# First modulations from whole fp32 weights as the stationary operand, with the conditioning rows prepared at the beginning

## Chip, cores and metric

One core of a Trainium2 chip. The metric is the device time of one execution in microseconds; the kernel before takes 1435.6 us, the median of 3 runs (1433.16 to 1436.79). Engines are named as in the profile: PE (matrix engine; PEld are its weight loads), DVE, ACT, POOL, and SP, which here only issues transfers.

## The reference, cut to what matters

Two layers over 256 latent tokens and 256 context tokens of width 1024. Each layer begins with a norm modulated by six vectors that come from the conditioning:

```python
def adaln(cond, w_ada, b_ada):
    return jnp.split(jax.nn.silu(cond) @ w_ada + b_ada, 6, axis=-1)

def modulate(x, shift, scale):
    return rms_norm(x) * (1.0 + scale) + shift

# per layer l
sh1, sc1, g1, sh2, sc2, g2 = adaln(c, w_ada[l], b_ada[l])
csh1, csc1, cg1, csh2, csc2, cg2 = adaln(c_ctx, w_ada[l], b_ada[l])
... = project(modulate(ctx, csh1, csc1), w_in[l])
... = project(modulate(x, sh1, sc1), w_in[l])
# three mixers (gating MLP, windowed attention, gated linear attention), merged, then
x_new = x + g1 * merge_branches(a_out, b_out, c_out, gates, w_br[l], w_o[l])
x_new = x_new + g2 * sq_relu_ffn(modulate(x_new, sh2, sc2), w_ff1[l], w_ff2[l])
```

`w_ada[l]` is 1024 x 6144. The change concerns the first 2048 of these columns in layer 0 (shift `sh1` and scale `sc1`), for both conditioning vectors.

## The kernel before

**Weights.** All weights stream from one packed tensor `wpk` in chunks of at most 128 x 1024 fp32 (512 KB), in the order of `layer_chunks`; `START_ORDER` is its beginning. A "B" chunk holds two 128-row blocks of 512 columns, an "A" chunk eight 128-row blocks of one column tile of 128. `emit_chunk` issues the transfer on SP's queue into a raw tile (two rings of four, the second used by the chunks of `START_RAW`), casts it to fp32r on ACT (`whi`, L296) and takes the rest on DVE or POOL (`wlo`, L298). `chunk` hands a split chunk to the matmuls and emits `SPLIT_AHEAD` = 2 further ones. Activations are split in the same way, and a product is three matmuls (hi x hi, hi x lo, lo x hi). Every matmul has the one line 316, every transpose line 320.

**Order.** The orders of PE and SP are those in which the program is written. A small planner writes them: `run` advances the main generator, which adds each matmul's estimated time to `clk`, and interleaves spawned generators when `clk` has reached their due time (the `LAT` table). ACT, DVE and POOL are ordered by Tile's scheduler.

**The start of layer 0** (`start`). SP issues the two x transfers, then raw chunks. `norm_start0` squares x on ACT, adds on DVE, sums over partitions on PE with `ones`, takes the power on POOL, spreads it by PE, and multiplies x by it in place (L1304, half on DVE, half on POOL). Meanwhile `ada_group` computes 512 columns of the modulation at a time from four "B" chunks: the stationary operand is `csil` (128 x 4: the two silu vectors, each split), the moving one the split weights with 512 columns, 16 matmuls a group, 64 in all. The result has four rows; `ada_rows` combines and transposes it with the small matrix `comb` (four fp32 matmuls, eight instructions a group) and adds the bias. Groups 0 and 1 give the first half of shift and scale, 2 and 3 the second. `half(i)` waits for them and for both norms, then modulates and splits four of the eight blocks of h (`nt`, L1361 and L1363; `h`, L367 and L368). Then the first projections (`kvp`, `qp`) run: kv and the two context query tiles with the first half of h, the same with the second, then the two latent query tiles. After that stand `load_constants2`, `layer_params` (masks, norms' gains, rope tables) and, last, `cond_rows`: it loads both conditioning vectors to all partitions (`sil`, 1 MB) and takes their silu (tanh on ACT, L467, two DVE steps, L468 and L469) through two tiles of the raw ring.

**Later modulations.** All other columns of both layers come from `ada_task`, background work on DVE: a row-wise product of `w_adaT` with `sil`, summed (L490).

**The query chain** (`q_chain`) takes a projected query tile through a square (ACT), a sum (DVE L665), a power (POOL L375), two products, a split (L676, L677), and PE's transposes, which stand in PE's order between the projections.

Of the kernel before, what the change touches and what calls it, by code (L numbers as in the profile page):

```python
# [16 lines left out]
P = 128  # L17
# [20 lines left out]
def layer_chunks(l):  # L38
# [38 lines left out]
    for kind, g, js in FFN_ORDER:  # L77
# [4 lines left out]
        else:  # L82
            for _ in range(2 if g == 3 and not last else 1):
# [8 lines left out]
             (1, 3, range(4)), (2, 2, None), (1, 3, range(4, 8)), (2, 3, None)]  # L92
LAT_FIRST = 4
# [50 lines left out]
def shape_constants():  # L144
    t = np.arange(SEQ)
    nf = HD // 4
    freqs = (10000.0 ** (-np.arange(nf, dtype=np.float32) / nf)).astype(np.float32)
    cos = np.zeros((SEQ, HD), np.float32)
    sin = np.zeros((SEQ, HD), np.float32)
    for half, pos in ((0, t // GRID_W), (1, t % GRID_W)):  # L150
        ang = pos.astype(np.float32)[:, None] * freqs[None, :]
        c, s = np.cos(ang), np.sin(ang)
        o = half * 32
        cos[:, o:o + nf] = c
        cos[:, o + nf:o + 2 * nf] = c
# [27 lines left out]
    comb = np.array([[1, 0], [0, 1], [1, 0], [0, 1]], np.float32)  # L183
    return {"rope": np.ascontiguousarray(rope.astype(np.float32)),
            "consts": np.ascontiguousarray(big), "comb": comb,
            "tri": np.ascontiguousarray(tri.transpose(1, 0, 2).reshape(P, -1))}
# [4 lines left out]
       "ada": 1.51, "x": 0.54, "half": 1.35, "kv_lat": 6.0, "kv_ctx": 4.5, "kv_out": 0.7, "q_lat": 7.5,  # L191
# [3 lines left out]
       "c_out": 1.5, "acc": 3.5, "rstd": 2.5, "rstd0": 0.77, "mod": 2.0,  # L195
# [11 lines left out]
class Builder:  # L207
# [76 lines left out]
    def emit_chunk(self):  # L284
# [8 lines left out]
        nc.sync.dma_start(raw[:, :n], src)  # L293
        hi = self.wp.tile([P, 1024], F32R, tag="whi", name="whi")
# [96 lines left out]
    def load_constants(self):  # L391
# [9 lines left out]
        self.comb = cp.tile([4, 2], F32, name="comb")  # L401
        nc.scalar.dma_start(self.comb, a["comb"])
# [44 lines left out]
    def cond_setup(self):  # L447
        nc, cp, a = self.nc, self.cp, self.a

        cT = self.tr(name="cT")[:, :16].rearrange("p (k c) -> p k c", c=2)  # L450
        nc.sync.dma_start(cT, a["condT"])
        th = self.tr(name="cth")[:, :16]
# [31 lines left out]
    def ada_task(self, l, n, conds):  # L484
# [3 lines left out]
        for c in conds:  # L488
            junk = self.bp.tile([P, D], BF16, tag="b2k", name="junk")
            nc.vector.scalar_tensor_tensor(junk, raw, 1.0, self.sil[:, c], op0=ALU.mult, op1=ALU.mult,  # L490
# [793 lines left out]
    def norm_start0(self, s, x, R):  # L1284
# [11 lines left out]
        yield self.lat("x")  # L1296
# [5 lines left out]
        for i in range(2):  # L1302
            xh = x[:, i * 4:i * 4 + 4, :]
            (nc.vector if i == 0 else nc.gpsimd).tensor_tensor(  # L1304
                xh, xh, R.unsqueeze(1).to_broadcast([P, 4, SEQ]), op=ALU.mult)
        self.flags.add(f"R{s}")

    def ada_group(self, g):
        c0 = ADA_START[g]
        ps = self.sc_bank()  # L1310
        for kc in range(4):
            if kc > 0:
                yield
            w = self.chunk(("B", "w_ada", c0, 512, 2 * kc))
            for kk in range(2):
                k = 2 * kc + kk
                for q in range(2):
                    self.mm(ps[:4, :], self.csil[:, k, :], w[q][:, kk * 512:(kk + 1) * 512],
                            start=(k == 0 and q == 0), stop=(k == KT - 1 and q == 1))
        rows = self.tp.tile([4, 512], F32, tag="t2k", name="adarow")  # L1320
        self.nc.scalar.copy(rows, ps[:4, :])
        self.spawn(self.ada_rows(g, rows), self.lat("ada"))

    def ada_rows(self, g, rows):

        nc = self.nc
        out = self.sc_bank()
        ov = out[:, :8].rearrange("p (n c) -> p n c", c=2)
        for j in range(4):
            self.mm(ov[:, j, :], rows[:, j * P:(j + 1) * P], self.comb, True, True)  # L1330
        n0 = ADA_START[g] // P
        o = self.ada[0][:, :, n0:n0 + 4]
        b = self.bada[:, 0, n0:n0 + 4].unsqueeze(1).to_broadcast([P, 2, 4])
        nc.vector.tensor_tensor(o, ov.rearrange("p n c -> p c n"), b, op=ALU.add)
        if n0 >= 8:
            nc.vector.tensor_scalar(o, o, 1.0, None, op0=ALU.add)
        self.flags.add(f"ada{g}")
        yield 0.0

    def start(self, h, kv_ready, q_ready):  # L1340
# [5 lines left out]
        ada = [self.ada_group(g) for g in range(4)]  # L1346
        for s in range(2):
            nc.sync.dma_start(x[s], self.a["xT"][s])
# [3 lines left out]
        yield from ada[0]  # L1352
        yield from ada[1]
        def half(i):
            yield from self.until(f"ada{2 * i}", f"ada{2 * i + 1}", "R0", "R1")
# [12 lines left out]
        self.spawn(half(0), 0.0)  # L1368
        yield from ada[2]
        yield from ada[3]  # L1370
# [20 lines left out]
        self.spawn(half(1), 0.0)  # L1391
# [5 lines left out]
        self.load_constants2()  # L1397
        self.layer_params(0)
# [5 lines left out]
        self.cond_rows()  # L1404
# [63 lines left out]
```

## Time and profile before

| | |
|---|---|
| median of 3 runs | 1435.6 us (1433.16 to 1436.79) |
| profiled execution | 1438.17 us, its span 1436.4 us |
| mean granted clock of PE | 0.979 |
| PE / PEld busy | 1366.7 (95%) / 1192.3 us |
| DVE / ACT / POOL busy | 991.7 (69%) / 661.6 (46%) / 451.7 us (31%) |
| moved by DMA | 214.08 MB, mean 149 GB/s |

The span runs from the first to the last instruction; what lies around it is 1.8 us here. Busy time of an engine is the union of its instructions. A granted clock of 1.00 is 2.4 GHz and 0.50 is 1.2 GHz. In a row of the timeline the first number is the start, the second the length of a merged run of equal instructions, and brackets tell the idle time before it and who ended it. In a table of stretches each engine's busy time is followed by its count of instructions.

### The profile page before, as it was taken

The numbers are of one execution on the slowest core, as the hardware profiler recorded it, in microseconds if no ns is written. First come the engines' busy times: TensorE is split into PE (matmuls) and PEld (weight loads), VectorE is DVE, ScalarE is ACT, GpSimd is POOL, SyncE is SP. The second block draws the span as 40 slices with busy tenths as digits, with TensorE's granted clock in tenths as the row PEclk, the third lists the DMA queues.
The fourth block names the chain that finished last, engine by engine and source line by source line (L and its number), as shares of the span: only waits on it lengthen the run. The fifth ranks groups of instructions, "written<-read, shape, count | busy, mean of one in ns | idle before, by whom it ended". The sixth has DMA issues, their size and how long they took to land.

```text
span 1436.4 us, 21724 instructions
## 1 busy us (share of the span) xinstructions
PE 1366.7 (95%) x8272; PEld 1192.3 (83%) x8272; DVE 991.7 (69%) x1669; ACT 661.6 (46%) x1095; POOL 451.7 (31%) x288
## 2 busy tenths in 40 slices
PE   4968998998999999999999999999999999999999
PEld 2757787877788889888887888987799999999999
DVE  7776678876576768768885566886875665864453
ACT  5755455643223335442332323555556635565443
POOL 2030002213112334553342424431110245465554
PEclk8989999998999999999999999999999999999999
DMA  7621112321354455444556656442144335556554
GB/s 301 230 73 45 59 64 68 118 103 45 118 175 162 150 196 182 158 140 172 205 207 213 216 193 215 165 149 89 48 138 149 104 118 161 180 162 202 181 178 131
DMA packets 60391, 214.08 MB, mean 149 GB/s; under 512 B 7230, under 2 KB 8510, under 8 KB 59648
## 3 DMA queue, kind: packets, MB, share of 16 engines
q1 hardware_dynamic: 58696, 209.51, 43.5%
q10 hardware_dynamic: 1592, 3.20, 0.7%
q8 instruction: 65, 1.06, 0.3%
q14 instruction: 38, 0.31, 0.1%
HBM read 211.63 MB, written 1.05 MB: 148 GB/s over the span
## 4 chain that ended last, share of the span: by engine, by line
PE 41%; DVE 10%; issue 3%; DMA 3%; ACT 1%; POOL 0%; SPq 0%; DVEq 0%; ACTq 0%; POOLq 0%
PE mm L316 37%; DVE junk L490 4%; DMA adaw<-w_adaT 3%; PE sm L316 2%; DVE wlo L298 1%; PE sc L316 1%; PE sm L320 1%; DVE acc L507 1%; ACT whi L296 0%; DVE h L546 0%; DVE x L1259 0%; DVE f L1215 0%; DVE mx L717 0%; DVE nt L541 0%; ACT gab L820 0%
## 5 line engine op out<-in xcount | busy, mean ns | idle before, releaser
L296 ACT CAST whi<-raw 128x1024 fp32r<-128x1024 f32 (+1 forms) x312 | 322.9, 1039 | 524.1 <-PE mm L316 419.0
L316 PE MATMUL mm<-h,whi 128*128 128x512 f32 (+2 forms) x2112 | 515.1, 336 | 1.7 <-ACT h L1177 0.8
L316 PEld LDWEIGHTS mm<-h,whi 128*128 128x128 f32 x2112 | 361.7, 192 | 40.8 <-DVE h L1178 1.1
L298 DVE TENSOR_TENSOR wlo<-raw,whi 128x1024 fp32r<-128x1024 f32 (+1 forms) x215 | 286.7, 1336 | 107.9 <-ACT whi L296 106.7
L316 PE MATMUL mm<-h,wlo 128*128 128x512 f32 (+2 forms) x1056 | 352.4, 334 | 0.0
L298 POOL TENSOR_TENSOR wlo<-raw,whi 128x1024 fp32r<-128x1024 f32 x97 | 240.1, 2475 | 346.7 <-ACT whi L296 340.9
L316 PE MATMUL mm<-f,whi 128*128 128x256 f32 (+1 forms) x1152 | 257.2, 319 | 0.0
L490 DVE SCALAR_TENSOR_TENSOR junk<-adaw,sil 128x1024 bf16<-128x1024 f32 x128 | 184.9, 1472 | 57.0 <-DMA adaw<-w_adaT 56.8
L316 PEld LDWEIGHTS mm<-h,wlo 128*128 128x128 f32 x1056 | 202.2, 192 | 19.2
L316 PEld LDWEIGHTS mm<-f,whi 128*128 128x128 f32 x1152 | 192.0, 191 | 15.2
L316 PE MATMUL mm<-f,wlo 128*128 128x256 f32 (+1 forms) x576 | 183.8, 319 | 2.9 <-DVE wlo L298 2.4
L316 PE MATMUL mm<-whi,h 128*128 128x512 f32 (+2 forms) x544 | 172.0, 386 | 0.0
L316 PEld LDWEIGHTS mm<-f,wlo 128*128 128x128 f32 x576 | 109.7, 190 | 11.7 <-DVE wlo L298 3.7
L316 PEld LDWEIGHTS mm<-whi,h 128*128 128x128 f32 x544 | 103.7, 199 | 16.3
L316 PE MATMUL mm<-wlo,h 128*128 128x512 f32 (+2 forms) x272 | 102.9, 378 | 0.4 <-DVE wlo L298 0.4
L1214 POOL TENSOR_TENSOR ffr<-ffr 128x512 f32<-128x512 f32 (+1 forms) x64 | 71.5, 1118 | 46.1 <-ACT f L1213 37.5
L1215 DVE TENSOR_TENSOR f<-ffr,f 128x512 fp32r<-128x512 f32 (+1 forms) x64 | 56.2, 886 | 29.7 <-POOL ffr L1214 29.5
L1259 DVE SCALAR_TENSOR_TENSOR x<-mm,ada,x 128x256 f32<-128x256 f32 x96 | 43.6, 478 | 42.5 <-PE mm L316 42.3
L383 POOL TENSOR_SCALAR gx<-gx 128x512 f32<-128x512 f32 (+1 forms) x14 | 14.0, 1000 | 183.2 <-ACT gx L382 183.1
L316 PE MATMUL mm<-m,whi 128*128 128x256 f32 x384 | 69.5, 283 | 0.0
L316 PEld LDWEIGHTS mm<-wlo,h 128*128 128x128 f32 x272 | 54.2, 199 | 8.1 <-DVE wlo L298 1.1
L1061 POOL TENSOR_TENSOR mg<-mg,gth 128x512 f32<-128x512 f32 (+1 forms) x28 | 34.4, 1230 | 84.1 <-DVE gth L1060 84.1
(291 smaller groups left out, 1828.5 us busy)
## 6 DMA issues: line engine op xcount, KB each, us to landing
raw<-wpk SPq DMA_DIRECT2D x304, 512.0 KB, 3.8
adaw<-w_adaT SPq DMA_DIRECT2D x80, 512.0 KB, 3.8
raw<-wpk SPq DMA_DIRECT2D x8, 288.0 KB, 2.9
x<-xT SPq DMA_DIRECT2D x2, 1024.0 KB, 6.9
x<-xT ACTq DMA_DIRECT2D x2, 1024.0 KB, 6.9
sil<-cond SPq DMA_DIRECT2D x1, 1024.0 KB
out<-x ACTq DMA_DIRECT2D x8, 128.0 KB, 1.7
trif<-tri SPq DMA_DIRECT2D x2, 384.0 KB, 2.9
```

The costliest lines, as they stand in the source:

```text
L296: nc.scalar.copy(hi[:, :n], raw[:, :n])
L298: eng.tensor_tensor(lo[:, :n], raw[:, :n], hi[:, :n].bitcast(F32), op=ALU.subtract)
L316: self.nc.tensor.matmul(out, lhsT, rhs, start=start, stop=stop)
L320: self.nc.tensor.transpose(out, src, self.ident)
L383: nc.gpsimd.tensor_scalar(x2[:, :n], x2[:, :n], 0.044715, 1.0, op0=ALU.mult, op1=ALU.add)
L490: nc.vector.scalar_tensor_tensor(junk, raw, 1.0, self.sil[:, c], op0=ALU.mult, op1=ALU.mult, accum_out=self.ada[l][:, c, n:n + 1])
L507: nc.vector.tensor_tensor(acc, acc, sq, op=ALU.add)
L1061: (nc.vector if m is not None and n >= KT - 2 else nc.gpsimd).tensor_tensor(mg, mg, th[:, :nt], op=ALU.add)
L1214: nc.gpsimd.tensor_tensor(r[:, :nt], r[:, :nt], r[:, :nt], op=ALU.mult)
L1215: nc.vector.tensor_tensor(lo, r[:, :nt], hi.bitcast(F32), op=ALU.subtract)
L1259: nc.vector.scalar_tensor_tensor(x[s][:, n], ps[:, s * SEQ:(s + 1) * SEQ], self.ada[l][:, s, 40 + n:41 + n], x[s][:, n], op0=ALU.mult, op1 ...
```

## The change

1. The first 2048 columns of the modulation arrive as sixteen "A" chunks, one column tile each. They are not split: `emit_chunk` keeps the raw tile. The raw weights become the stationary operand (128 x 128 fp32), `csil` in fp32 (two columns) the moving one: eight matmuls a tile, and the result stands already with columns on partitions. `ada_rows` and `comb` go.
2. `ada_half` takes eight tiles for the first half of shift and scale and eight for the second; each adds its bias in two DVE steps.
3. SP issues two raw chunks ahead of each x transfer.
4. x is scaled by its norm in `half(i)`, four blocks at a time and on DVE alone.
5. `cond_rows`, `load_constants2` and `layer_params` are called after the first eight tiles; `cond_rows` works in four pieces of 512 through other tiles, and its factor 0.5 moves into `ada_task`.
6. The planner's due times for these steps are new.

```diff
-ADA_START = (0, 1024, 512, 1536)
+ADA_START = ((0, 1, 2, 3, 8, 9, 10, 11), (4, 5, 6, 7, 12, 13, 14, 15))
-START_ORDER = [("B", "w_ada", c0, 512, kk) for c0 in ADA_START[:2] for kk in range(0, KT, 2)]
-START_ORDER += [("B", "w_ada", c0, 512, kk) for c0 in ADA_START[2:] for kk in range(0, KT, 2)]
+START_ORDER = [("A", "w_ada", 0, n * P) for ns in ADA_START for n in ns]
...
         nc.sync.dma_start(raw[:, :n], src)
+        if self.specs[i][1] == "w_ada":
+            self.split[i] = raw
+            return
...
     def cond_setup(self):
-        self.csil = self.big([P, KT, 4], F32R, name="csil")
-        self.split_hl(self.csil[:, :, 0:2], self.csil[:, :, 2:4], thv)
+        self.csil = thv
...
     def cond_rows(self):
         for c in range(2):
-            th = self.wp.tile([P, D], F32, tag="raw", bufs=4, name="silt")
-            nc.scalar.activation(th, self.sil[:, c], AF.Tanh, scale=0.5)
-            nc.vector.scalar_tensor_tensor(th, th, 1.0, self.sil[:, c], op0=ALU.add, op1=ALU.mult)
-            nc.vector.tensor_scalar(self.sil[:, c], th, 0.5, None, op0=ALU.mult)
+            for i in range(2):
+                v = self.sil[:, c, i * 512:(i + 1) * 512]
+                th = self.trb(name="silt")
+                nc.scalar.activation(th, v, AF.Tanh, scale=0.5)
+                nc.vector.scalar_tensor_tensor(v, th, 1.0, v, op0=ALU.add, op1=ALU.mult)
...
     def norm_start0(self, s, x, R):
         nc.scalar.copy(R, R0[:, :SEQ])
-        for i in range(2):
-            xh = x[:, i * 4:i * 4 + 4, :]
-            (nc.vector if i == 0 else nc.gpsimd).tensor_tensor(
-                xh, xh, R.unsqueeze(1).to_broadcast([P, 4, SEQ]), op=ALU.mult)
...
-    def ada_group(self, g):
-    def ada_rows(self, g, rows):
+    def ada_half(self, i):
+        nc = self.nc
+        ps = self.sc_bank()
+        ov = ps[:, :16].rearrange("p (n c) -> p n c", c=2)
+        for j, n in enumerate(ADA_START[i]):
+            w = self.chunk(("A", "w_ada", 0, n * P))
+            for k in range(KT):
+                self.mm(ov[:, j], w[:, k * P:(k + 1) * P], self.csil[:, k], k == 0, k == KT - 1)
+            self.clk += ADA_TILE
+            yield
+        for j in (0, 4):
+            n0 = ADA_START[i][j]
+            o = self.ada[0][:, :, n0:n0 + 4]
+            b = self.bada[:, 0, n0:n0 + 4].unsqueeze(1).to_broadcast([P, 2, 4])
+            r = ov[:, j:j + 4].rearrange("p n c -> p c n")
+            if j == 0:
+                nc.vector.tensor_tensor(o, r, b, op=ALU.add)
+            else:
+                nc.vector.scalar_tensor_tensor(o, r, 1.0, b, op0=ALU.add, op1=ALU.add)
+        self.flags.add(f"ada{i}")
...
     def start(self, h, kv_ready, q_ready):
         for s in range(2):
+            for _ in range(2):
+                self.emit_chunk()
             nc.sync.dma_start(x[s], self.a["xT"][s])
...
         def half(i):
-            yield from self.until(f"ada{2 * i}", f"ada{2 * i + 1}", "R0", "R1")
+            yield from self.until(f"ada{i}", "R0", "R1")
+            for s in range(2):
+                xh = x[s][:, i * 4:i * 4 + 4, :]
+                nc.vector.tensor_tensor(xh, xh, Rs[s].unsqueeze(1).to_broadcast([P, 4, SEQ]), op=ALU.mult)
...
+        for i in range(2):
+            yield from self.ada_half(i)
+            self.spawn(half(i), self.lat("ada"))
+            if i == 0:
+                self.cond_rows()
+                self.load_constants2()
+                self.layer_params(0)
         yield from self.need("half0")
```

The calls of `ada[0]` to `ada[3]`, and the later calls of `load_constants2`, `layer_params` and `cond_rows`, go from their old places.

## Rows read from the trace of the kernel before

**Rows 1.** The page: busy time of each engine, share of the span, instructions

```profile
PE 1366.7 (95%) x8272; PEld 1192.3 (83%) x8272; DVE 991.7 (69%) x1669; ACT 661.6 (46%) x1095; POOL 451.7 (31%) x288
```

**Rows 2.** Busy time by stretch: us, each engine (instructions), granted clock, DMA share, GB/s

```profile
2.00:47.66 45.66, 27.72 (x105) 12.80 (x105) 34.26 (x45) 28.01 (x40) 8.03 (x4) 0.89 0.79 291
47.66:79.30 31.64, 31.21 (x177) 27.01 (x175) 24.65 (x52) 21.88 (x41) 1.39 (x2) 1.00 0.53 191
79.30:92.30 13.00, 6.01 (x19) 5.07 (x19) 8.43 (x17) 4.58 (x10) 5.85 (x2) 0.61 0.29 98
```

**Rows 3.** Groups by line, 0 to 47.4 us: count, busy us, mean ns, idle before

```profile
L298 DVE TENSOR_TENSOR wlo<-raw,whi 128x1024 fp32r<-128x1024 f32 x16 | 19.3, 1220 | 3.2 <-ACT whi L296 3.2
L296 ACT CAST whi<-raw 128x1024 fp32r<-128x1024 f32 x16 | 16.3, 1043 | 12.7 <-PE sc L316 12.7
L1304 DVE TENSOR_TENSOR x<-x,Rb 128x1024 f32<-128x1024 f32 x2 | 6.7, 3402 | 0.0
```

**Rows 4.** Timeline of the first 40 us: start, length, engine, line, operation, count

```profile
1.18 0.90 SPq L1348 DMA_DIRECT2D x<-xT  x2
7.04 2.19 ACT L1290 ACTIVATE sq<-x 128x512 f32<-128x512 f32 x4 [3.14 <-DMA x<-xT]
11.73 2.93 ACT L296 CAST whi<-raw 128x1024 fp32r<-128x1024 f32 x3
```

**Rows 5.** Timeline, weight loads of 128x128 fp32 (PEld), then matmuls with two moving columns

```profile
15.80 0.76 PEld L316 LDWEIGHTS sm<-ones,sq 128*128 128x128 f32 x3
...
16.66 0.55 PEld L316 LDWEIGHTS sm<-ones,sq 128*128 128x128 f32 x2
...
30.20 1.86 PE L316 MATMUL sc<-comb,adarow 4*128 4x2 f32 x8
32.00 0.59 PE L316 MATMUL sc<-whi,csil 128*4 128x512 f32 x1
```

**Rows 6.** Timeline of PE, loads of 128x128 with two moving columns, in dense work

```profile
340.33 0.25 PE L316 MATMUL sm<-ind,gh 128*128 128x2 f32 x1
...
340.89 0.25 PE L316 MATMUL sm<-ind,gl__2775 128*128 128x2 f32 x1
```

**Rows 7.** Busy time by stretch, two stretches around rises of the clock

```profile
30.70:34.12 3.42, 3.42 (x13) 1.89 (x13) 1.65 (x3) 0.87 (x2) 0.00 (x0) 0.50 0.92 274
354.84:358.40 3.56, 3.56 (x9) 2.81 (x9) 3.53 (x15) 0.76 (x2) 0.00 (x0) 0.50 0.00 0
```

**Rows 8.** Timeline of PE, small matmuls and then dense ones, 351 to 359 us

```profile
351.82 3.09 PE L316 MATMUL sm<-v,glaw 64*128 64x128 f32 x16
354.84 1.22 PE L316 MATMUL mm<-h,whi 128*128 128x512 f32 x2
...
358.42 0.44 PE L316 MATMUL mm<-h,wlo 128*128 128x512 f32 x1
```

**Rows 9.** Timeline around the first kv matmul and of the second half of h

```profile
47.66 0.30 PE L316 MATMUL mm<-whi,h 128*128 128x288 f32 x1
...
50.75 1.05 PE L316 MATMUL sc<-comb,adarow 4*128 4x2 f32 x8
53.52 0.17 DVE L1336 TENSOR_SCALAR ada<-ada 128x8 f32<-128x8 f32 x1
...
58.66 2.50 DVE L368 TENSOR_TENSOR h<-nt,h 128x512 fp32r<-128x512 f32 x4
```

**Rows 10.** Timeline, the first context q chain and PE's wait for it

```profile
77.12 0.68 DVE L665 TENSOR_REDUCE qss<-qt 128x8 f32<-128x512 f32 x1
...
79.56 4.21 POOL L375 TENSOR_TENSOR rq<-rq,mhalf 128x8 f32<-128x8 f32 x1 [6.77 <-DVE rq L374]
...
86.32 1.94 PE L320 MATMUL sm<-ident,qt 128*128 128x128 f32 x8 [6.99 <-DVE qt L677]
```

**Rows 11.** Groups by line of DVE, 73.4 to 82.5 us

```profile
L468 DVE SCALAR_TENSOR_TENSOR silt<-silt,sil 128x1024 f32<-128x1024 f32 x2 | 2.4, 1220 | 0.0
L469 DVE TENSOR_SCALAR sil<-silt 128x1024 f32<-128x1024 f32 x2 | 1.4, 686 | 0.0
```

More of the change, by code (lines that the diff above doesn't have):

```diff
@@ L182, in shape_constants @@
     ], 1).astype(np.float32)
-    comb = np.array([[1, 0], [0, 1], [1, 0], [0, 1]], np.float32)
     return {"rope": np.ascontiguousarray(rope.astype(np.float32)),
-            "consts": np.ascontiguousarray(big), "comb": comb,
+            "consts": np.ascontiguousarray(big),
             "tri": np.ascontiguousarray(tri.transpose(1, 0, 2).reshape(P, -1))}
 LAT = {
-       "ada": 1.51, "x": 0.54, "half": 1.35, "kv_lat": 6.0, "kv_ctx": 4.5, "kv_out": 0.7, "q_lat": 7.5,
+       "ada": 0.5, "x0": 6.5, "x1": 11.0, "half": 3.0, "kv_lat": 6.0, "kv_ctx": 4.5, "kv_out": 0.7, "q_lat": 7.5,
        "q_ctx": 5.0, "q_out": 1.0, "s_lat": 4.2, "s_ctx": 3.4, "p_lat": 2.6, "p_ctx": 2.0, "po": 1.0,
@@ L194 @@
        "g2": 1.5, "g3": 1.0, "g1s": 3.0, "g4": 1.8, "1g4": 7.0, "states": 8.0, "on": 4.0, "c": 1.2,
-       "c_out": 1.5, "acc": 3.5, "rstd": 2.5, "rstd0": 0.77, "mod": 2.0,
+       "c_out": 1.5, "acc": 3.5, "rstd": 2.5, "rstd0": 3.0, "mod": 2.0,
        "0states": 15.2, "0s_lat": 2.83, "0mix": 1.68, "1acc": 4.66, "1s_lat": 3.91, "0g2": 1.26, "0va0": 5.01,
@@ L400, in load_constants @@
         nc.vector.memset(self.mhalf, -0.5)
-        self.comb = cp.tile([4, 2], F32, name="comb")
-        nc.scalar.dma_start(self.comb, a["comb"])
         self.ada = [cp.tile([P, 2, 48], F32, name=f"ada{l}") for l in range(DEPTH)]
@@ L448, in cond_setup @@
         nc, cp, a = self.nc, self.cp, self.a
-        cT = self.tr(name="cT")[:, :16].rearrange("p (k c) -> p k c", c=2)
+        cT = cp.tile([P, 16], F32, name="cT").rearrange("p (k c) -> p k c", c=2)
         nc.sync.dma_start(cT, a["condT"])
-        th = self.tr(name="cth")[:, :16]
+        th = cp.tile([P, 16], F32, name="cth")
         thv = th.rearrange("p (k c) -> p k c", c=2)
@@ L489, in ada_task @@
             junk = self.bp.tile([P, D], BF16, tag="b2k", name="junk")
-            nc.vector.scalar_tensor_tensor(junk, raw, 1.0, self.sil[:, c], op0=ALU.mult, op1=ALU.mult,
+            nc.vector.scalar_tensor_tensor(junk, raw, 0.5, self.sil[:, c], op0=ALU.mult, op1=ALU.mult,
                                            accum_out=self.ada[l][:, c, n:n + 1])
@@ L1295, in norm_start0 @@
         nc.vector.tensor_tensor(acc[:, :SEQ], acc[:, :SEQ], acc[:, SEQ:], op=ALU.add)
-        yield self.lat("x")
+        yield self.lat(f"x{s}")
         st = self.sm_bank()
@@ L1301, in norm_start0 @@
         nc.scalar.copy(R, R0[:, :SEQ])
-        for i in range(2):
-            xh = x[:, i * 4:i * 4 + 4, :]
-            (nc.vector if i == 0 else nc.gpsimd).tensor_tensor(
-                xh, xh, R.unsqueeze(1).to_broadcast([P, 4, SEQ]), op=ALU.mult)
         self.flags.add(f"R{s}")
-    def ada_group(self, g):
-        c0 = ADA_START[g]
+    def ada_half(self, i):
+        nc = self.nc
         ps = self.sc_bank()
[L1311 to L1322, printed above, removed]
@@ L1324, in ada_rows @@
-    def ada_rows(self, g, rows):
[L1326 to L1338, printed above, removed]
+        ov = ps[:, :16].rearrange("p (n c) -> p n c", c=2)
@@ L1345, in start @@
         x = [self.big([P, KT, SEQ], name="x") for s in range(2)]
-        ada = [self.ada_group(g) for g in range(4)]
         for s in range(2):
+            for _ in range(2):
+                self.emit_chunk()
             nc.sync.dma_start(x[s], self.a["xT"][s])
@@ L1351, in start @@
         yield
-        yield from ada[0]
-        yield from ada[1]
         def half(i):
-            yield from self.until(f"ada{2 * i}", f"ada{2 * i + 1}", "R0", "R1")
+            yield from self.until(f"ada{i}", "R0", "R1")
+            for s in range(2):
+                xh = x[s][:, i * 4:i * 4 + 4, :]
+                nc.vector.tensor_tensor(xh, xh, Rs[s].unsqueeze(1).to_broadcast([P, 4, SEQ]), op=ALU.mult)
             for k in range(4 * i, 4 * i + 4):
@@ L1366, in half @@
             self.flags.add(f"half{i}")
-        self.spawn(half(0), 0.0)
-        yield from ada[2]
-        yield from ada[3]
+        for i in range(2):
[5 more added lines that the diff above has]
+                self.layer_params(0)
         yield from self.need("half0")
@@ L1390, in start @@
             yield from kvp(kk)
-        self.spawn(half(1), 0.0)
         for kk in (0, 2):
@@ L1396, in start @@
             yield from kvp(kk)
-        self.load_constants2()
-        self.layer_params(0)
         kv_ready(ps["kv"])
```

2 lines of the change are left out of this document (1 added, 1 removed).

## The prediction

> **What bounds the kernel now.** The page comes first: PE is busy for 95% of the span [rows 1], so PE's order of work is the clock of the whole kernel, and an edit is worth what it moves on PE. The edits here lie in one stage, so the second view is busy time by stretch [rows 2]. Before the first projection matmul (47.66 us) PE has work in only 27.7 of 45.7 us; from 47.66 to 79.3 it is busy for 31.2 of 31.6 us; from 79.3 to 92.3 for 6.0 of 13 us, at a mean granted clock of 0.61. So two holes stand at the beginning: the modulation stage, and one near 80 us. The third view is the groups of the stage [rows 3]: the splitting of the 16 modulation chunks takes 19.3 us of DVE and 16.3 us of ACT, and the scaling of x takes another 6.7 us of DVE in two instructions of 3.4 us. PE waits for these, not they for PE. The last view is the timeline: where the stage begins [rows 4], where it ends [rows 9], and what PE waits for near 80 us [rows 10].
>
> All that follows is one question: at what time does PE reach the first kv matmul? Nothing after it in PE's order can begin earlier, and from there PE is nearly full.
>
> **The change, part by part.**
>
> *The matmuls of the stage.* Removed are 64 matmuls of 512 moving columns, the rows of combined results and their 32 small matmuls. Added are 16 column tiles of 8 fp32 matmuls, each with a new 128x128 stationary tile and two moving columns. An fp32 matmul is two instructions in this trace: the sums of squares (`sm<-ones,sq`, four calls) are 8 weight loads and 8 matmuls, with a stationary operand of the same form and one moving column. So the stage gets 16 x 8 x 2 = 256 load-and-matmul pairs; the 8 calls of the two norms that stand among them make 16 more, 272 in all. With two moving columns the weight load is the price. Rows show it at both levels of the clock. One load of this form starts at 15.80 and the fourth after it at 16.66 us: 0.86 us for four, 0.215 us each; the eight pairs with `comb` take 30.20 to 32.00, 0.225 us each, at a granted clock of 0.5, that is 1.2 GHz [rows 5]. Later, at 2.4 GHz, six pairs with two moving columns start from 340.33 to 340.89, five steps of 0.112 us [rows 6]. (The clock column shows 1.00 until about 27 us, but loads at 15.8 us run at the pace of those at 0.5; I take the pace.) The stage costs 272 x 0.215 = 58.5 us at the lower level, and 272 x 0.112 = 30.5 us at the upper.
>
> The Trainium skill ("TensorE: Matmul & The Clock Gate", section "LDWEIGHTS (loading the stationary operand)") gives a load as its columns over 1.2 in ns, 107 ns for 128 columns, with no word of the clock's level. By it the pairs would take an estimated 29 us wherever the clock stands, and the stage would end near 34 us. The rows agree with it at the upper level only, and at the lower one they show twice that.
>
> *Which level?* The engine starts at the lower one, and I look at what it did before it rose. From 30.70 to 34.12 PE is busy without a hole, 1.3 us of it with the small `comb` pairs, and the clock stays at 0.50 [rows 7]. From 351.82 sixteen small matmuls run without a hole for 3.0 us, at a pace set by weight loads, and after them the dense matmuls begin still at half pace [rows 8]; 3.56 us of dense matmuls of 512 columns follow at 0.50 [rows 7], and only then, near 358.4, the pace doubles. So weight loads with little to stream do not lift the clock in these rows, and the new stage has nothing else. I take the lower level for the whole stage: 58.5 us.
>
> *When it begins.* Now the x transfers go first; two of them are issued at 1.18 us and the first has landed at 7.04 [rows 4]. After the change half a megabyte of weights is first in the queue, so the first tile can start between 3 and 7 us; I take 5.0. It no longer waits for ACT's split (11.73). Transfers do not bind: the stage moves at 291 GB/s on average [rows 2], 1.8 us for a chunk of 0.52 MB, against 16 x 0.215 = 3.4 us of PE for it. A chunk's buffer is now freed by PE, not by the split; with eight buffers that is a lead of seven tiles, some 24 us. End of the stage: 5.0 + 58.5 = 63.5 us, against 47.66: **+15.8 us**.
>
> *The clock at the first kv matmuls.* Before, the stage handed over a fast PE. Now the dense matmuls must lift it first: after 354.84 it took 3.58 us at half pace [rows 8], of which half is lost: **+1.8 us** (ends 0 and 3.4).
>
> *What leaves the kv and q work.* The last eight `comb` pairs stand inside it, 1.0 us [rows 9], and 0.4 us of its holes are waits for a split that is now long done [rows 2]: **-1.4 us**.
>
> *Splits, x scaling, the modulations' last step.* The 35.6 us of ACT and DVE work on the chunks go; nothing of that is gained again, as PE is the last to end in the new stage. The scaling of x leaves POOL and becomes DVE work in each half. The first half lies beside tiles 10 to 16, over 20 us. The second starts when PE ends: from the last modulation to the last part of h took 53.52 to 61.16, 7.6 us [rows 9], plus at most 6.7 us of scaling [rows 3], 14.3 us; 2.4 us if DVE is alone (its 1024-column operations take 1.2 us each [rows 3]), then 10. PE's cover is the first halves of kv and q: 13.5 us before (47.66 to 61.16), about 14 with the slow start. So nothing, or up to 1 us.
>
> *Conditioning rows, constants and layer parameters.* Their transfers, about 2 MB, go onto SP's queue ahead of the raw chunk of the eleventh tile: 7 us at 291 GB/s, behind which that chunk and all later ones stand. Its buffer comes free when tile 3 ends and it is due eight tiles later, some 27 us: covered. The activations (ACT) and products (DVE) go beside the tiles: free. What they leave is worth something. Near 73 to 82 us they were 2.4 + 1.4 = 3.8 us of DVE [rows 11], between the first query tile's steps: its sum at 77.12, the power on POOL from 79.56 for 4.21 us, and PE's wait of 7.0 us, ending at 86.32, for the end of that chain [rows 10]. I take the whole 3.8 us as earlier: **-3.8 us**. The ends are 0, if the scheduler puts other splits there, and -10, if the wait goes and the clock with it does not fall (6.0 us of PE work at mostly half pace [rows 2]).
>
> *Sum:* 15.8 + 1.8 - 1.4 - 3.8 = **+12.4 us**. The profiled execution took 1438.2 us (a span of 1436.4 and 1.8 outside it), which gives 1450.6; it was 2.6 us above the median of the three runs, 1435.6. Against that median: **1448 us**, 0.9% slower.
>
> **The rivals.**
>
> *The clock rises in the stage* (the other side). If PE full of weight loads counts as work, the pairs run at 0.112 us, and transfers and pairs come near each other: 12.5 MB at 291 GB/s would end near 45 us, pairs alone at 5.0 + 30.5, near 36. Taking 40, kv starts 7.7 us earlier, on a fast PE: -7.7 - 1.4 - 3.8 = -12.9, **1423 us**. It decides as soon as the stage ends before about 51 us, where the later gains of 5.2 balance its loss and the slow start. The Trainium skill (the same page, section "What's actually happening") says that the throttled state is the default and activity releases it; it leaves open there whether a load is such activity. For it: the stretches I have of this kind are short [rows 7, 8]. Against it: both are full of PE work, and neither lifts the clock.
>
> *Faster loads at the lower level.* Sixteen pairs with 64 rows in the stationary operand take 3.02 us, 0.189 us each [rows 8]. Then the stage takes 51.4 us, kv starts 8.7 us later, and the sum is 8.7 + 1.8 - 1.4 - 3.8 = +5.3, **1441 us**. Against it: the loads at 0.215 us have the very form of the new ones [rows 5].
>
> *The later gain does not come.* Tile orders ACT, DVE and POOL anew; if the q chain keeps its wait and the second half of h is 1 us late, the sum is 15.8 + 1.8 - 1.4 + 1 = +17.2, **1453 us**.
>
> **How the numbers follow.** Forecast 0.74; clock rises 0.12; faster loads 0.08; no later gain 0.06. The forecast's own range, from the start's 2 us either way, 0.225 us a pair (+2.7), the ends of the q chain and some 2 us of a changed order further down, is 1440 to 1456. To hold 8 times in 10 I take 1438 to 1456: it leaves out the risen clock and tails of the others, 0.20. A measurement of this kernel can tell about 0.3%, 4.3 us: faster (under 1431.3) 0.12, within 0.08, slower (over 1439.9) 0.80.
>
> **What would show it.** Right: the granted clock at 0.5 or loads 0.21 us apart through the whole stage, PE without holes in it, the first kv matmul at 60 to 67 us, 3 to 4 us of dense matmuls at half pace, and a q wait under 4 us. Wrong: loads 0.11 us apart before 40 us, or kv before 51 us; PE holes for raw chunks would mean that transfers, not loads, are the price.

## The result, and the profile after

The changed kernel takes 1447.4 us, the median of 4 runs (1444.9 to 1451.7). The kernel before, run beside it, took 1434.4 us (4 runs, 1432.5 to 1436.8). The ratio is 1.0095, with a 95% interval of 1.0072 to 1.0119: about 1% slower. The profiled execution of the changed kernel has a span of 1449.9 us, 13.5 us more than that of the kernel before (1436.4).

The page of the changed kernel, busy time of each engine:

```profile
PE 1400.5 (97%) x8432; PEld 1242.3 (86%) x8432; DVE 970.0 (67%) x1652; ACT 643.9 (44%) x1076; POOL 445.4 (31%) x286
```

Beside [rows 1], PE is busy 33.8 us more, its loads (PEld) 50 us more, and DVE 22, ACT 18 and POOL 6 us less. The change took work from the three engines that have time to spare and gave work to the one that has none.

The timeline of PE in the changed kernel (start, length, line, operation, count; brackets: idle time before, and who ended it). Line 316 of before is 319 here, and the transposes are L323:

```profile
4.71 13.79 PE L319 MATMUL sc<-cth,raw 128*128 128x2 f32 x64 [4.71 <-DMA raw<-wpk]
18.36 0.99 PE L319 MATMUL sm<-ones,sq 128*128 128x1 f32 x4
19.21 6.97 PE L319 MATMUL sc<-cth,raw 128*128 128x2 f32 x32
26.04 1.20 PE L319 MATMUL sm<-dg,ones 128*128 128x128 f32 x4
27.03 0.85 PE L319 MATMUL sm<-ones,sq 128*128 128x1 f32 x4
27.74 6.97 PE L319 MATMUL sc<-cth,raw 128*128 128x2 f32 x32
34.57 1.20 PE L319 MATMUL sm<-dg,ones 128*128 128x128 f32 x4
35.56 27.31 PE L319 MATMUL sc<-cth,raw 128*128 128x2 f32 x128
62.73 0.59 PE L319 MATMUL mm<-whi,h 128*128 128x288 f32 x1
...
67.44 0.42 PE L319 MATMUL mm<-wlo,h 128*128 128x288 f32 x1
67.68 0.45 PE L319 MATMUL mm<-whi,h 128*128 128x288 f32 x2
...
97.22 1.07 PE L323 MATMUL sm<-ident,qt 128*128 128x128 f32 x8 [2.82 <-DVE qt L678]
```

All 272 pairs of the stage are in the first eight rows, 256 of the new kind and 16 of the two norms (eight of these, `sm<-dg,ones`, stream 128 columns), one run behind the other without a hole. The pace is read from starts: 128 pairs from 35.56 to 62.73 us are 0.2123 us each, 64 from 4.71 to 18.36 us 0.2133. The first kv matmul stands at 62.73 us, against 47.66 [rows 9]; 20 matmuls from there to 67.68 us are 0.24 us apart, and those behind 0.133. Then the wait for the first query tile is 2.82 us, against 6.99 [rows 10].

Busy time by stretch of the changed kernel (length; PE, PEld, DVE, ACT, POOL, each with its count of instructions; granted clock; DMA share; GB/s):

```profile
2.00:62.73 60.73, 58.02 (x272) 58.05 (x273) 21.54 (x44) 14.29 (x27) 4.80 (x2) 1.00 0.73 270
62.73:94.40 31.67, 31.66 (x169) 28.42 (x169) 18.92 (x39) 17.96 (x34) 3.03 (x3) 1.00 0.35 114
97.22:122.60 25.38, 20.60 (x102) 16.43 (x103) 18.37 (x58) 14.56 (x36) 6.91 (x7) 0.93 0.19 63
...
323.50:482.00 158.50, 154.26 (x755) 125.97 (x755) 99.69 (x151) 45.59 (x66) 34.66 (x25) 0.95 0.39 122
482.00:1429.30 947.30, 927.63 (x5991) 840.80 (x5990) 645.27 (x1014) 432.28 (x677) 359.30 (x214) 0.99 0.52 165
```

The first two rows answer to [rows 2]: in the stage PE's loads run for 58.05 us and PE waits only for the first chunk (2.0 to 4.71); DVE falls from 34.3 to 21.5 us, ACT from 28.0 to 14.3. From 62.73 to 94.40 PE has no hole. The column of the clock has to be read with care: it shows 1.00 for both stretches, although the stage runs at half pace and the first 4.95 us after it are slow too. In this trace the column shows a lower value only from the first fall that was recorded; before it, the pace of equal instructions is what tells the level.

The last three rows are later places with the same work on either side. Their counterparts in the kernel before:

```profile
86.32:115.80 29.48, 23.70 (x102) 18.70 (x103) 18.68 (x58) 15.36 (x37) 8.32 (x7) 0.84 0.11 36
...
316.70:472.40 155.70, 151.18 (x756) 123.25 (x756) 99.72 (x151) 45.60 (x67) 34.68 (x25) 0.97 0.38 124
472.40:1415.80 943.40, 924.43 (x5991) 837.86 (x5990) 645.72 (x1014) 432.07 (x677) 357.78 (x214) 0.99 0.50 166
```

From the transposes of the first query tile to the first product of the softmax with V (97.22 to 122.6 us here, 86.32 to 115.8 there) the changed kernel is 4.1 us quicker: the mean clock is 0.93 instead of 0.84, and PE is busy 3.1 us less for the same 102 matmuls. From 323.5 to 482.0 it takes 158.5 us for the work (755 or 756 matmuls, as the cut falls) that took 155.7 before, and from there to the output 947.3 against 943.4. So the lead of the old kernel is 6.8 us at the first product with V (122.6 against 115.8), still 6.8 at 323.5 us (316.7 there), 9.6 at 482.0 us (472.4), and 13.5 us at the output (1429.3 against 1415.8).

Behind 482 us the mean clock is 0.99 on both sides, so shorter stretches must tell. Two places of the changed kernel where it falls:

```profile
1115.00:1145.00 30.00, 27.94 (x205) 26.32 (x203) 18.64 (x38) 20.28 (x34) 5.17 (x4) 0.89 0.36 106
1250.00:1280.00 30.00, 28.55 (x221) 27.93 (x220) 20.90 (x39) 17.19 (x29) 16.57 (x11) 0.94 0.52 159
```

Their counterparts in the kernel before:

```profile
1105.00:1135.00 30.00, 27.94 (x216) 26.23 (x215) 19.41 (x38) 20.43 (x35) 6.28 (x7) 0.94 0.37 107
1240.00:1270.00 30.00, 28.56 (x233) 27.94 (x233) 21.69 (x40) 18.12 (x31) 17.14 (x13) 1.00 0.55 177
```

PE is busy for the same time and does fewer matmuls. As an estimate from these rows, 30 us x 0.05 and 30 us x 0.06 are 3.3 us of PE's time at full speed, of the 3.9 us that are lost there.

### The profile page after: what moved, and what is told of

It is laid out like the page before. It is cut to its first block, busy times and chain, and to the rows that moved or that the text cites. A ratio compares the mean times of both kernels' runs of the same rounds, so it can differ in the third digit from the quotient of the medians.

```text
span 1449.9 us, 21963 instructions
## 1 busy us (share of the span) xinstructions
PE 1400.5 (97%) x8432; PEld 1242.3 (86%) x8432; DVE 970.0 (67%) x1652; ACT 643.9 (44%) x1076; POOL 445.4 (31%) x286
## 4 chain that ended last, share of the span: by engine, by line
PE 38%; DVE 10%; DMA 5%; issue 3%; ACT 1%; POOL 0%; SPq 0%; DVEq 0%; ACTq 0%; POOLq 0%
PE mm L319 34%; DMA adaw<-w_adaT 5%; DVE junk L491 5%; DVE wlo L301 2%; PE sm L319 2%; PE sc L319 1%; PE sm L323 1%; DVE acc L508 1%; ACT whi L299 0%; DVE x L1260 0%; DVE h L547 0%; DVE mx L718 0%; DVE f L1216 0%; DVE nt L542 0%; ACT gab L821 0%
## 5 line engine op out<-in xcount | busy, mean ns | idle before, releaser
L299 ACT CAST whi<-raw 128x1024 fp32r<-128x1024 f32 (+1 forms) x296 | 306.8, 1040 | 525.7 <-PE mm L319 422.8
L301 DVE TENSOR_TENSOR wlo<-raw,whi 128x1024 fp32r<-128x1024 f32 (+1 forms) x199 | 265.2, 1333 | 116.6 <-ACT whi L299 115.6
L491 DVE SCALAR_TENSOR_TENSOR junk<-adaw,sil 128x1024 bf16<-128x1024 f32 x128 | 193.4, 1538 | 57.5 <-DMA adaw<-w_adaT 57.3
L319 PEld LDWEIGHTS mm<-f,whi 128*128 128x128 f32 x1152 | 192.0, 191 | 15.1
L1216 DVE TENSOR_TENSOR f<-ffr,f 128x512 fp32r<-128x512 f32 (+1 forms) x64 | 51.8, 818 | 29.6 <-POOL ffr L1215 29.6
L319 PEld LDWEIGHTS mm<-m,whi 128*128 128x128 f32 x384 | 59.9, 192 | 0.1
```

The source lines that it names most:

```text
L299: nc.scalar.copy(hi[:, :n], raw[:, :n])
L301: eng.tensor_tensor(lo[:, :n], raw[:, :n], hi[:, :n].bitcast(F32), op=ALU.subtract)
L319: self.nc.tensor.matmul(out, lhsT, rhs, start=start, stop=stop)
L491: nc.vector.scalar_tensor_tensor(junk, raw, 0.5, self.sil[:, c], op0=ALU.mult, op1=ALU.mult, accum_out=self.ada[l][:, c, n:n + 1])
L1216: nc.vector.tensor_tensor(lo, r[:, :nt], hi.bitcast(F32), op=ALU.subtract)
```

## The experiments

The theory: a stage of weight loads with two moving columns is full of PE work and still does not lift the clock, so each load costs twice its price. The rivals: PE's work lies elsewhere (other steps of the change, transfers), or the load has that price whatever the clock does.

**The same loads with 128 moving columns.** The two silu columns are repeated 64 times in the moving operand. The loads, chunks and order stay, and PE has 64 times as many columns to stream. `ADA_TILE`, the planner's estimate of a tile, is lowered by as much, so that its order stays.

```diff
+ADA_COLS = 128
...
-                self.mm(ov[:, j], w[:, k * P:(k + 1) * P], self.csil[:, k], k == 0, k == KT - 1)
+                self.mm(ps[:, 2 * j:2 * j + ADA_COLS], w[:, k * P:(k + 1) * P],
+                        self.csil[:, k].unsqueeze(1).to_broadcast([P, ADA_COLS // 2, 2]), k == 0, k == KT - 1)
```

> The changed kernel, but each modulation matmul streams 128 moving columns (the two silu columns repeated 64 times) instead of 2; the 126 surplus results are overwritten by the next tile or never read. Same weight loads, same transfers, same order. Theory (the stage is paced by loads at the lower clock, because PE streams almost nothing): at half clock 128 fp32 columns fit beside a load (128 columns twice at 1.2 GHz is 0.213 us), so nothing is lost, and with PE streaming the clock rises within the first tiles; pairs then start 0.11 to 0.12 us apart, the stage ends near 38 to 42 us instead of 62.7, the first kv matmul is fast, and the kernel takes 1420 to 1426 us. Rival 1 (the clock stays low for another reason, as the start of the program or fp32 weight loads themselves): pairs stay at 0.213 us, kv at 62 to 64 us, 1447 us. Rival 2 (columns come on top of loads): pairs at 0.3 us or more, kv later than 80 us, over 1465 us.

Measured: 1424.3 us (4 runs, 1419.4 to 1426.9), 0.9905 of the kernel before (0.9878 to 0.9931). More work for PE made the kernel 23 us faster than the changed one. Timeline of PE in this kernel:

```profile
4.82 5.96 PE L320 MATMUL sc<-cth,raw 128*128 128x128 f32 x32 [4.82 <-DMA raw<-wpk]
11.07 3.84 PE L320 MATMUL sc<-cth,raw 128*128 128x128 f32 x32 [0.28 <-DMA raw<-wpk]
...
16.12 3.84 PE L320 MATMUL sc<-cth,raw 128*128 128x128 f32 x32 [0.88 <-DMA raw<-wpk]
...
30.07 10.98 PE L320 MATMUL sc<-cth,raw 128*128 128x128 f32 x96 [1.62 <-DMA raw<-wpk]
40.81 0.38 PE L320 MATMUL mm<-whi,h 128*128 128x288 f32 x1
```

The first 32 pairs take 5.96 us, 0.186 each; from then on 32 take 3.84 (0.12 each), and the last 96 stand from 30.07 to 40.81, 0.112 each, which is the price at the upper level [rows 6]. The first kv matmul is at 40.81 us, and there is no slow start behind it (its first matmul takes 0.38 us, not 0.59). This is what the theory had expected (kv at 38 to 42 us, 1420 to 1426 us). So the load itself is not slow; the clock was. PE's waits for raw chunks in the first 45 us (total, times, longest):

```profile
PE sc L320 <- DMA raw<-wpk: 7.6, 4, 4.8
```

4.8 of the 7.6 us are the wait for the first chunk; the other three holes, 2.8 us together, say that transfers now end close behind the loads.

**128 columns in the first eight tiles only, two in the last eight.** Does a clock that is up stay up under loads?

```diff
+        cols = ADA_COLS if i == 0 else 2
...
+                self.mm(ps[:, 2 * j:2 * j + cols], w[:, k * P:(k + 1) * P],
+                        self.csil[:, k].unsqueeze(1).to_broadcast([P, cols // 2, 2]), k == 0, k == KT - 1)
```

> The changed kernel with 128 moving columns in the first eight tiles and 2 in the last eight. Theory (weight loads with two columns neither raise nor hold the clock): the first half runs as with 128 columns throughout and ends near 25 us; in the second half the granted clock falls to 0.50 and pairs go to 0.21 us, kv starts near 50 to 53 us on a slow clock, 1433 to 1438 us. Rival (once risen, PE that is full of loads holds the clock): pairs stay at 0.11 us, kv near 41 us, 1423 to 1426 us.

Measured: 1430.4 us (8 runs, 1424.3 to 1433.6), 0.9959 (0.9934 to 0.9984). Timeline of PE in this kernel:

```profile
21.09 3.82 PE L320 MATMUL sc<-cth,raw 128*128 128x128 f32 x32
24.75 0.61 PE L320 MATMUL sm<-dg,ones 128*128 128x128 f32 x4
25.19 25.16 PE L320 MATMUL sc<-cth,raw 128*128 128x2 f32 x128
50.21 0.59 PE L320 MATMUL mm<-whi,h 128*128 128x288 f32 x1
```

Busy time by stretch of the same kernel (columns as above):

```profile
20.00:25.00 5.00, 5.00 (x47) 5.00 (x47) 3.31 (x7) 0.37 (x1) 1.63 (x1) 1.00 1.01 380
25.00:30.00 5.00, 4.91 (x38) 4.82 (x36) 4.38 (x12) 3.19 (x7) 0.00 (x0) 0.78 0.98 378
30.00:50.21 20.21, 20.21 (x96) 20.21 (x96) 8.23 (x15) 6.20 (x10) 0.00 (x0) 0.50 0.77 276
```

Eight tiles with two columns begin at 25.19 us on a fast clock. In the next stretch the granted clock falls, and from 30 us to the end of the stage it is 0.50 (1.2 GHz), while PE and PEld are busy without a hole. The 128 pairs take 25.0 us, where 128 x 0.112 would be 14.3, and the first kv matmul is slow again (0.59 us). Here the column names the level that in the changed kernel could be read only from the pace. So long runs of loads with two columns neither lifted the clock here nor held it, as the theory had expected; the total, 1430.4 us, came out 2.6 us below its 1433 to 1438. Why the chip grants as it does the runs cannot say.

**Half of the loads.** The matmuls of every second block of k are left out, and with them half of the sum; all transfers stay.

```diff
-            for k in range(KT):
-                self.mm(ov[:, j], w[:, k * P:(k + 1) * P], self.csil[:, k], k == 0, k == KT - 1)
+            for k in range(0, KT, 2):
+                self.mm(ov[:, j], w[:, k * P:(k + 1) * P], self.csil[:, k], k == 0, k == KT - 2)
```

> The changed kernel with every second 128-row block of the first modulations left out (four matmuls a tile instead of eight), so with 128 load-and-matmul pairs fewer; all transfers remain. Theory (PE's weight loads are the stage): 128 x 0.213 = 27 us less, kv near 36 us, 1419 to 1422 us. Rival (transfers or the buffers that PE frees are close behind the loads): kv not before 42 us, 1426 us or more.

Measured: 1423.1 us (2 runs), 0.9908 (0.9874 to 0.9942); the first kv matmul at 40.44 us, between what the theory (near 36) and its rival (not before 42) had said. PE's waits for raw chunks in this kernel (total, times, longest):

```profile
PE sc L319 <- DMA raw<-wpk: 9.0, 4, 5.5
```

5.5 us are the wait for the first chunk, and three holes of 3.5 us come on top of 144 pairs x 0.2123 = 30.6 us: together 39.6. Of the 27.2 us of loads that were taken out (128 x 0.2123), 22.3 us arrived at the first kv matmul. So the price of the stage is that of its loads, down to about 40 us, where PE begins to wait for the transfers.

**The conditioning rows, constants and parameters at their old places.** The rest of the change stays. This was run twice, in two sets of runs, and the changed kernel was run again in the second.

```diff
-            if i == 0:
-                self.cond_rows()
-                self.load_constants2()
-                self.layer_params(0)
...
             yield from kvp(kk)
+        self.load_constants2()
+        self.layer_params(0)
...
         q_ready((yield from self.proj_b("w_in", C_QB, 512, h, [0, 1])))
+        self.cond_rows()
```

> The changed kernel with the conditioning rows, the constants and the layer parameters called at their old places (after the second kv part and after the projections). Theory (their early place frees DVE in the query chain): kv starts at 62.7 us as before, PE's wait before the first query transposes grows from 2.8 to about 7 us and the clock falls in it; 4 to 8 us slower than the changed kernel, 1451 to 1456 us. Rival (the early place gives nothing, the shorter wait comes from something else, as the splits that are gone or a new order by the scheduler): the wait stays near 3 us, 1446 to 1449 us.

> The changed kernel once more, unaltered. Question: the profiled execution stood 6.8 us behind the kernel before at the first product of probabilities and values, and 13.5 us at the output. Theory (between them PE has the same work, and the clock falls at other places in each execution): kv again at 62.7 and that first product at 122 to 123 us within 0.5 us, but the stretches at a granted clock of 0.50 after 130 us lie elsewhere or are of other lengths, and the span differs by 1 to 5 us with them. Rival (the program sets them): the same stretches within 1 us.

> The changed kernel with conditioning rows, constants and parameters at their old places, once more and beside the changed kernel on the same chip. Its first product of probabilities and values was 5.5 us later than that of the changed kernel, its median only 0.7 us. Theory (the 5 us are real and the rest is where the clock falls): again 5 to 6 us later at that product, and 2 to 6 us in the median against the changed kernel run beside it. Rival (later work catches the 5 us up): the same lag there and a median within 1.5 us.

Measured: 1448.2 us (4 runs), 1.0094 (1.0066 to 1.0121), and 1449.6 us (4 runs), 1.0111 (1.0063 to 1.0158); the changed kernel again 1448.3 us (4 runs), 1.0093 (1.0060 to 1.0127). The medians with late rows are 0.7 and 1.3 us above those of the changed kernel, where 4 to 8 us and then 2 to 6 us had been expected: in all, the early rows are worth nothing that these runs can tell. But where they act, they act: the transposes of the first query tile stand after a wait of 5.26 us, not 2.82 (timeline of PE, rows at the old places):

```profile
99.57 1.94 PE L323 MATMUL sm<-ident,qt 128*128 128x128 f32 x8 [5.26 <-DVE qt L678]
```

The first step of that chain, the tile's sum, in the changed kernel:

```profile
89.11 0.68 DVE L666 TENSOR_REDUCE qss<-qt 128x8 f32<-128x512 f32 x1
```

The sum and the power on POOL with the rows at the old places:

```profile
92.95 0.68 DVE L666 TENSOR_REDUCE qss<-qt 128x8 f32<-128x512 f32 x1
95.39 1.64 POOL L378 TENSOR_TENSOR rq<-rq,mhalf 128x8 f32<-128x8 f32 x1 [5.56 <-DVE rq L377]
```

PE's wait begins at the same time in both (94.40 and 94.31 us). With early rows the sum comes 3.8 us earlier, as the prediction had it, and 2.4 us of that reach PE. Against the kernel before, the wait is 1.7 us shorter even with late rows (5.26 against 6.99): there the power on POOL took 4.21 us [rows 10], and it takes 1.64 us in both kernels here. What made it long there no run shows.

The products with V, as a group (count; fastest, median and slowest in ns; first to last in us), in the changed kernel:

```profile
L319 PE MATMUL sm<-PT,V x160: 277/280/384, 122.6 to 1069.8; 128*128 128x256 f32 x160
```

The same group in the changed kernel's second run:

```profile
L319 PE MATMUL sm<-PT,V x160: 277/280/387, 122.8 to 1069.9; 128*128 128x256 f32 x160
```

In the kernel with late rows:

```profile
L319 PE MATMUL sm<-PT,V x160: 277/280/390, 128.1 to 1066.1; 128*128 128x256 f32 x160
```

And in its second run:

```profile
L319 PE MATMUL sm<-PT,V x160: 277/280/390, 127.5 to 1064.1; 128*128 128x256 f32 x160
```

The first product comes at 122.6 and 122.8 us with early rows, and at 128.1 and 127.5 with late ones: 5 us, twice. And where these 5 us go, busy time by stretch of the second kernel with late rows shows:

```profile
328.20:480.60 152.40, 148.13 (x756) 120.91 (x756) 100.52 (x151) 45.59 (x67) 34.67 (x25) 0.99 0.42 127
```

This is the work that takes 158.5 us in the changed kernel (whose second run has a clock of 0.95 there too): 152.4 us, at a granted clock of 0.99, in both runs with late rows. So in these profiled executions the clock between 324 and 482 us gives back what the early rows had won.

Whether the early rows bring on these falls is not shown. That falls come at other places in each execution had been expected of the repeated changed kernel, and its two profiled executions did not bear it out: their cold stretches stand at the same places within 1 us, up to the end. But both are the slowest run of their four (1451.7 and 1451.6 us, mean clock 0.981); the other six runs of the changed kernel show a mean clock of 0.982 to 0.987, so fewer or shorter falls. The two profiled executions with late rows differ from one another (spans of 1446.1 and 1441.0 us). And a kernel that is met below as the best version ran in two profiled executions with spans of 1421.4 and 1414.4 us. The same 40 us, in the first and in the second of them:

```profile
320.00:360.00 40.00, 38.02 (x187) 31.83 (x184) 28.05 (x54) 13.44 (x21) 8.78 (x7) 0.87 0.29 93
```

```profile
320.00:360.00 40.00, 38.00 (x222) 31.06 (x221) 29.79 (x56) 14.11 (x23) 9.27 (x8) 1.00 0.33 106
```

So in this part of the kernel some falls belong to the execution and not to the program.

**Early rows in the kernel before.** Only the calls of `cond_rows` (in its new form), `load_constants2` and `layer_params` move, to behind the first two groups.

```diff
         yield from ada[0]
         yield from ada[1]
+        self.cond_rows()
+        self.load_constants2()
+        self.layer_params(0)
```

> The kernel before with one part of the change alone: conditioning rows (in their four new pieces), constants and layer parameters called after the first two modulation groups; modulations as before. Theory: kv starts within 3 us of 47.7 us, the query wait shrinks from 7 to about 3 us; 4 to 8 us faster than the kernel before, 1427 to 1431 us. Rival (in the old stage DVE is what PE waits for, so 2.6 us of products and the transfers ahead of later chunks delay the stage by as much as the query chain gains): kv starts 4 us later or more, 1433 to 1437 us.

Measured: 1437.3 us (10 runs, 1434.0 to 1439.3), 1.0006 (0.9992 to 1.0019): the same, as the rival had said. The wait of the first query tile is 2.82 us here too, but the first kv matmul comes at 52.61 us instead of 47.66. Busy time by stretch of this kernel (columns as above):

```profile
40.00:45.00 5.00, 4.02 (x11) 0.87 (x12) 4.37 (x10) 4.80 (x8) 0.00 (x0) 0.69 0.62 205
45.00:50.00 5.00, 4.35 (x16) 2.24 (x15) 4.80 (x8) 4.18 (x7) 0.00 (x0) 0.65 0.46 128
2.00:52.61 50.61, 32.03 (x105) 14.27 (x105) 40.80 (x60) 31.39 (x47) 8.02 (x4) 0.84 0.83 306
```

The same 10 us in the kernel before:

```profile
40.00:45.00 5.00, 4.69 (x23) 1.99 (x21) 4.51 (x9) 4.74 (x8) 0.00 (x0) 1.00 0.73 226
45.00:50.00 5.00, 3.85 (x21) 2.35 (x22) 4.39 (x8) 5.00 (x9) 0.00 (x0) 1.00 0.70 235
```

The rows bring DVE from 34.3 [rows 2] to 40.8 us in a stage where PE waits for splits, but PE's idle time grows by only 0.6 us (18.6 against 17.9). The larger part of the delay is the clock: the same 105 matmuls keep PE busy for 32.0 instead of 27.7 us, and between 40 and 50 us the clock stands at 0.69 and 0.65, not at 1.00. The gain behind is paid in front. In the new stage PE has no hole, and DVE and ACT have that time to spare.

**Toward a better version.** With 128 columns PE waits for transfers, so the next question was whether 2 MB of constants, parameters and rows should stand in front of the last tiles' chunks. First the constants and parameters alone go behind the second half:

```diff
             if i == 0:
                 self.cond_rows()
-                self.load_constants2()
-                self.layer_params(0)
+        self.load_constants2()
+        self.layer_params(0)
         yield from self.need("half0")
```

> The kernel with 128 moving columns in all tiles, and the constants and layer parameters (1 MB) called after the second half instead of after the first; the conditioning rows stay early. Theory (with fast pairs the transfers ahead of the raw chunks bind: PE waited 1.6 us for a chunk there): that wait goes, kv 1.5 to 3 us earlier than 40.8 us, the kernel 1421 to 1424 us. Rival (the pairs are the bound, the wait is caught up): kv within 1 us of 40.8.

> The kernel with 128 moving columns and late constants and parameters once more, for an interval. Theory: kv at 38.3 us within 1 us again, 1417 to 1423 us, a ratio to the kernel before of 0.986 to 0.991, clear of 1. Rival (the two runs so far were lucky in where the clock falls later): over 1425 us.

Measured: 1418.8 us (2 runs), 0.9895 (0.9842 to 0.9948), and again 1417.8 us (6 runs, 1415.8 to 1424.0), 0.9887 (0.9858 to 0.9917). Of the first 1421 to 1424 us had been expected; the second lies where it was expected. The first kv matmul in the latter, from PE's timeline:

```profile
38.67 0.38 PE L320 MATMUL mm<-whi,h 128*128 128x288 f32 x1
```

And PE's waits for raw chunks there (total, times, longest):

```profile
PE sc L320 <- DMA raw<-wpk: 6.5, 2, 5.6
```

5.6 of the 6.5 us are the wait for the first chunk, so one hole of 0.9 us is left of three, and kv comes 2.1 us earlier than with all three calls in front. This is the best version that ran, 1.1% under the kernel before; its interval overlaps that of the first one with 128 columns, so that of the two the better is shown by the trace of the stage, not by the total.

With `cond_rows` moved behind the second half as well:

```diff
-            if i == 0:
-                self.cond_rows()
-                self.load_constants2()
-                self.layer_params(0)
+        self.cond_rows()
+        self.load_constants2()
+        self.layer_params(0)
```

> 128 moving columns, and the conditioning rows too (1 MB) after the second half, so that nothing but x and raw chunks is transferred ahead of the last tile. Theory (transfers were still close behind the pairs): kv 0.5 to 1.5 us earlier than 38.3 us, but the products of the rows now lie on DVE beside the second half of h and the first splits; total within 3 us of the other, 1416 to 1423 us. Rival (DVE beside the second half delays h or the query chain): PE's wait before the first query transposes grows past 4 us, 1424 us or more.

Measured: 1422.9 us (7 runs), 0.9931 (0.9904 to 0.9959); kv at 38.84 us, no earlier, and the wait of the first query tile 2.82 us, no longer. The first product with V comes at 96.9 us, against 97.2 with early rows. Yet the median is 5.1 us above that of the version before, where 3 us at most had been expected; the profiled executions lose it behind that product (the last product with V at 1040.6 against 1035.8 us). Whether the rows' place does this or the falls of the clock in these executions is not shown.

## Why the prediction was right, and where it was not

1448 us was forecast and 1447.4 measured, inside the range; the medians differ by 13.0 us. Term by term, from the two profiled executions:

| term | predicted | measured |
|---|---|---|
| the stage begins at | 5.0 us | 4.71 us |
| one pair | 0.215 us | 0.2123 us |
| first kv matmul | +15.8 us (63.5) | +15.1 us (62.73) |
| slow start | +1.8 us | +2.3 us (20 matmuls, 4.95 us) |
| kv and q work | -1.4 us | -2.3 us |
| first query tile's wait | -3.8 us | -4.2 us (-2.4 by the early rows) |
| from there to the first product with V | 0 | -4.1 us |
| from there to the output | 0, "some 2 us" | +6.7 us |
| sum | +12.4 us | +13.5 us |

The fifth term: 62.73 to 94.40 is 31.67 us with 2.3 us of slow start in it (20 matmuls at 0.24 instead of 0.133 us), and it was 31.64 without [rows 2].

*The stage.* This step carried the forecast, and it held in both factors: 272 pairs, and the lower level throughout. The loads at 15.80 us gave the price within 2%, the `comb` pairs within 6% [rows 5], and the two short stretches full of PE work that left the clock where it was [rows 7, 8] stood for one of 58 us. To go from 3 us to 58 was a bet ("the stretches I have of this kind are short"), and it came out. The experiment with 128 columns shows the cause: with the same loads a pair fell to 0.112 us, the pace of the upper level, and the time came near the rival's figure for a clock that rises (1424.3 against 1423 us, kv at 40.81 against 40). The Trainium skill ("TensorE: Matmul & The Clock Gate", section "LDWEIGHTS (loading the stationary operand)") gives a load as its columns over 1.2 in ns, 107 ns for 128. The runs agree at the upper level (0.112 us a pair) and show twice that at the lower (0.2123).

*The rival of faster loads* (0.189 us) fell by the same rows. *The rival of no later gain* fell too: the wait was 2.82 us. That transfers would not bind held, as PE had no hole for a chunk; with half of the loads, or at twice the pace, it had three each behind the first chunk (3.5 and 2.8 us).

*What was hidden.* The scaling of x and the second half of h cost nothing: no hole in PE from 62.73 to 94.40 us. The moved transfers cost nothing in the changed kernel either.

*What was misread.* "PE waits for these, not they for PE" holds only in part: in [rows 3] the casts on ACT themselves sat idle for 12.7 us until a matmul of PE ended. No term of the sum hangs on it. The wait of the first query tile came out in size, but not by the rows alone: 2.4 us are theirs, and the other 1.7 us came with a shorter power on POOL, which the sum did not have.

*What was mis-sized.* The forecast took everything behind the first query tile's wait for equal on both sides. It is not: 4.1 us are won before the first product with V, where the clock is low for a shorter time (the end of -10 us in the prediction was for this; wait and clock together gave -8.3), and 6.7 us are lost behind it. The two partly cancel, so that the total came out closer than its terms; that was luck. The loss was outside the text's "some 2 us of a changed order further down"; 2.8 us of it lie between 323.5 and 482.0 us, at a clock of 0.95 against 0.97. The other 3.9 us lie behind that, where PE is busy 3.2 us longer for the same 5991 matmuls; an estimated 3.3 us of it are the two falls at 1115 to 1145 and 1250 to 1280 us. So the loss is time at the lower clock. Both profiled executions took longer than the median of their kernel (1451.7 and 1438.2 us), and their difference, 13.5 us, is near that of the medians; a loss of this size is therefore likely in the others too, but where it falls there no trace shows, nor what in the change brings it on.

## What to carry to other kernels

Cost a long run of weight loads with few moving columns at the lower level of the clock, even where the clock is up when it begins (here it fell within 5 us), and cost the first dense work behind it at that level too (here 5 us of it); a busy PE is no sign of a fast one. Where a PE is bound so and the result has room, repeat the moving columns: the same loads at 128 columns took 36 us instead of 58, waits included. And a few us won early in a kernel that goes through falls of the clock count only when the median has moved: follow the gain to the end of the trace, and compare two executions of one kernel before a fall is put down to a change.

## What was not expected of the hardware

- A clock that was up fell under loads: with 128 columns in the first half of the stage and two in the second, the two-column loads began at 25.19 us with the clock at 1.00, and from 30 us on it stood at 0.50, with PE busy all the time.
- The column of the granted clock is 1.00 for the whole first 67 us of the changed kernel, while equal pairs take 0.2123 us, against 0.112 us later; in this trace it tells a level only behind the first fall.
- Falls of the clock can come back at the same places within 1 us in another execution of the same kernel (the changed one, 158.5 us from 323.5 to 482.0 us in both), and need not: the best version ran from 320 to 360 us at a clock of 0.87 in one execution and of 1.00 in another, and their spans differ by 7.0 us.
